# Two-layer convolution and retention block: paired projections computed by Strassen's seven products

## The chip, the cores and the metric

The kernel runs on one core of a Trainium2 chip. The metric is device time in microseconds from launch to end; a run's time is that of its slowest core, here the only one. TensorE (PE in the profile) multiplies, VectorE (DVE), ScalarE (ACT) and GpSimd (POOL) do elementwise work, and SyncE (SP) issues the transfers.

## The reference, cut to what matters

The program is two model blocks in one launch, all in float32, on 528 tokens (16 meta tokens and 512 of x) of 1024 features. The first block (attention and a gated recurrence, then a feed-forward part) is not touched. The second block runs two layers; in each, one wide projection of the normed input feeds a retention branch, a convolution branch and two gates:

```python
def _short_conv_branch(h, gb, gc, z, conv_w, conv_b, w_out):
    u = gc * h
    up = jnp.pad(u, ((0, 0), (CONV_WIDTH - 1, 0), (0, 0)))
    T = u.shape[1]
    y = conv_b + sum(conv_w[j] * up[:, j:j + T] for j in range(CONV_WIDTH))
    y = gb * y * jax.nn.silu(z)
    return y @ w_out
...
    for l in range(DEPTH_2):
        xn = _rmsnorm(h, pre_norm_g[l])
        proj = xn @ w_in[l] + b_in[l]
        c_h, c_b, c_c, c_z, r_q, r_k, r_v, r_z, g_a, g_b = jnp.split(proj, split_at, axis=-1)
        y_a = _short_conv_branch(c_h, c_b, c_c, c_z, conv_w[l], conv_b[l], w_conv_out[l])
        y_b = _retention_branch(r_q, r_k, r_v, r_z, ret_gn_g[l], w_ret_out[l])
        y = jax.nn.sigmoid(g_a) * y_a + jax.nn.sigmoid(g_b) * y_b
        y = y @ w_o[l]
        h = h + _rmsnorm(y, post_norm_g[l])
```

The convolution's four inputs (c_h, c_b, c_c, c_z) and the gates g_a and g_b are each 1024 features of `x_normed @ w_in + b_in`, so eight output tiles of 128 features apiece.

## The kernel before, in words

Activations lie transposed: features on the 128 partitions, tokens along the row, as eight "k tiles" of 128 features. A float32 product is made of three passes of TensorE's faster float32r form: every operand is split exactly in a high and a low part, and `mm3` adds high by high, high by low and low by high (L146 to L148). A **unit** is the weights of one output tile, 128 by 1024 numbers, 512 KB. `unit` (L123 to L125) loads it on SP's queue into one of three buffers `wraw`, ScalarE makes the high part `whi`, VectorE the low part `wlo` (three buffers each). These three instructions are given a priority 60 instructions ahead of where they stand. `proj` multiplies a unit by the tokens of a segment: 8 k tiles by 3 passes, 24 matmuls into one PSUM bank of the eight. `fproj` does so for each segment: in the first layer always two halves of 264 tokens; in the second, where the meta tokens' outputs don't count, one segment of 512, except for the two inputs of the convolution's product, which take segments of 258 and 256 tokens.

A planner (list scheduling at build time) sets the order on each engine: of the instructions whose inputs and buffers are ready it takes the one that stands first by priority, and it hands out whichever buffer of a kind is free. Semaphores then hold each engine to that order of its own.

Each layer has the retention branch first, then the stretch that the change touches, inside the pool `cv`: for each of eight convolution tiles four units (c_c, c_h, c_b, c_z) with their eviction (L1130 on ScalarE, L1136 on VectorE), the three-tap convolution on VectorE (L1138, L1140), the gates' products (L1145, L1149, L1150 on GpSimd) and the split of the result (L140, L141); then eight units g_b (sigmoid L1158 on ScalarE, product L1159 on GpSimd) and eight units g_a (L1163). After these the convolution's output projection (units `wc`, L1168 and L1169) is mixed with the retention output and split into the place of the layer's normed input `xs`, from which the last projection (`wo`) reads. In this stretch all is paced by the order of the projections on TensorE: 48 units per layer before `wc`. The first layer's stretch lies at 1223 to 1503 us of the profile, the second's at 2057 to 2325 us.

Of the kernel before, what the change touches and what calls it, by code (L numbers as in the profile page):

```python
# [7 lines left out]
F32 = mybir.dt.float32  # L8
# [29 lines left out]

# vector parameters: one column of 128 features each
# [18 lines left out]
class Builder:  # L58
# [5 lines left out]
    # ---------------------------------------------------------------- helpers  # L64
# [19 lines left out]
    # A chain is work whose steps wait for each other across the engines. It yields how many  # L84
    # projections to put on the tensor engine before its next step.
# [26 lines left out]
    def unit(self, src, pool=None):  # L112
        """One weight unit from DRAM, split exactly into two float32r parts; these stay in pool."""
        nc = self.nc
        cols = src.shape[-1]
        raw = self.wp.tile([P, 1040], F32, name="wraw", tag="wraw", bufs=3)[:, :cols]
        hi, lo = (
            (pool or self.wp).tile([P, 1024 if pool else 1040], F32R, name=f"w{n}", tag=f"w{n}", bufs=KEEP if pool else 3)[:, :cols]
            for n in ("hi", "lo")
        )  # L120
        # ahead of the work of the projections before it
        with self.tc.high_priority(offset=AHEAD):
            nc.sync.dma_start(raw, src)  # L123
# [13 lines left out]
    def split(self, hi, lo, src, eng=None):  # L137
        """src in two parts that float32r holds."""
# [4 lines left out]
    def mm3(self, out, w, x, start, stop):  # L143
        """out += w^T x from the exact two part splits of both."""
# [22 lines left out]
    def fproj(self, src, xs, segs, tick=True):  # L167
        """The same for a whole unit of 8 k tiles, for each segment of tokens."""
# [5 lines left out]

    def tokproj(self, xs, w0, us, n):
        """Rows of the token window at w0 times a chunk of n columns."""
# [26 lines left out]
    def metaproj(self, us, n):  # L203
        """The meta tokens' rows times a chunk."""
# [7 lines left out]
    def sqacc(self, acc, src, a, n, first, eng=None, last=False):  # L212
        """acc[:, a:a+n] (+)= src ** 2; the last square is returned instead of added."""
# [34 lines left out]
    def spread(self, r2, cols):  # L248
        """The same on all partitions, as a row, in PSUM."""
# [9 lines left out]
    def normed(self, src, g, dst, a, n, rb):  # L259
        """dst (hi, lo) = src times its norm factors rb times the weights g."""  # L260
# [13 lines left out]
    # ---------------------------------------------------------------- block 1  # L274
    def block1(self, stack):
# [4 lines left out]
        with tc.tile_pool(name="b1", bufs=1) as b1:  # L280
# [8 lines left out]
            # the attention's half of the output projection, by halves of the tokens: the first  # L289
            # half's norm runs under the second  # L290
# [16 lines left out]
    def out_proj(self, us, u, f, m, h, a, n):  # L307
        """h += an output tile of one branch's half of the output projection."""
# [4 lines left out]
    def mixer(self, b1, h, acc, mixh, fq, fk, lf8):  # L313
        """Both branches' outputs, before the output projection."""
# [7 lines left out]
        # h's place serves the recurrence's queries and gates until h is wanted  # L322
# [11 lines left out]
        rb = acc        # in its place, once the squares are summed  # L334
        W = [(w, P) for w in WIN1]
        with tc.tile_pool(name="lbp", bufs=1) as lp:
            # the input times the norm's weights; the norm's factors come with the projections' outputs
# [30 lines left out]
            # 1 - lower bound of the forget gate: cumsum(softmax over the one layer) - its first row  # L368
# [10 lines left out]
            for c in range(2):  # L379
# [3 lines left out]
                for t in (1, 2, 3, 4, 0):  # L383
# [13 lines left out]
                    for u, ps in todo:  # L397
# [4 lines left out]
                        # -f, away from 0  # L402
# [44 lines left out]
        # one step is a head's token tile; each runs in three stages, and projections between  # L447
        # them keep the tensor engine at work while the other engines are at a stage
# [74 lines left out]
    def hgrn_step(self, hc, hd, t, f, omf, V, qT, og, M, Mk, mask, mixh):  # L523
# [8 lines left out]
        if t < 4:  # L532
            # k of this tile, decayed to the tile's end
# [5 lines left out]
        if t > 0:  # L539
# [6 lines left out]
            for b in range(2):  # L546
# [6 lines left out]
                # level l's queries are the odd ones of the blocks of 64 >> l tokens, its keys the even ones  # L553
# [47 lines left out]
    def blocks(self, x, l, i):  # L601
        """The tile's blocks of 64 >> l tokens, every second from i."""
# [91 lines left out]
            # a step is a head's query tile: scores and softmax, later its transposes, then the head's output  # L694
# [51 lines left out]
    def fox_turn(self, t, hd, PT, PM, pt):  # L746
        """The tile's weights with the keys on the partitions."""
# [12 lines left out]
        if t == 3:  # L760
            # this tile meets only the last keys: their product goes whole
# [573 lines left out]
```

## Time and profile before

| | us |
|---|---|
| median of 3 runs (lowest, highest) | 2428.38 (2424.8, 2431.4) |
| span of the profiled execution | 2429.1 |
| TensorE busy in it | 2385.5 |
| VectorE busy | 1204.2 |
| ScalarE busy | 877.6 |
| GpSimd busy | 381.8 |

The span, from the first instruction to the last, is the profiled execution's own time; it lies 0.7 us above the median of the runs. Busy time counts the union of an engine's instructions. Matmuls are pipelined, so the durations of single matmuls overlap; what one costs is read from the distance between starts.

### The profile page before, as it was taken

The numbers are of one execution on the slowest core, as the hardware profiler recorded it, in microseconds if no ns is written. First come the engines' busy times: TensorE is split into PE (matmuls) and PEld (weight loads), VectorE is DVE, ScalarE is ACT, GpSimd is POOL, SyncE is SP. The second block draws the span as 40 slices with busy tenths as digits, with TensorE's granted clock in tenths as the row PEclk, the third lists the DMA queues.
The fourth block names the chain that finished last, engine by engine and source line by source line (L and its number), as shares of the span: only waits on it lengthen the run. The fifth ranks groups of instructions, "written<-read, shape, count | busy, mean of one in ns | idle before, by whom it ended". The sixth has DMA issues, their size and how long they took to land.

```text
span 2429.1 us, 38728 instructions
## 1 busy us (share of the span) xinstructions
PE 2385.5 (98%) x16130; PEld 2199.9 (91%) x16130; DVE 1204.2 (50%) x2131; ACT 877.6 (36%) x1522; POOL 381.8 (16%) x431
## 2 busy tenths in 40 slices
PE   8999989999999999999999999999999999999998
PEld 7888878888889999999999999999898888898888
DVE  5467776333337645455534323566455554443243
ACT  6333564222225434242422233454332323222223
POOL 3133442000004211110100020042110110001200
PEclk9999999999999999999999999999999999999999
DMA  4212103222334322222122222413222222222222
GB/s 159 90 33 67 62 20 120 95 93 93 94 120 165 109 88 74 82 79 87 62 96 87 93 91 87 131 66 116 82 81 86 87 83 73 93 96 96 96 87 70
DMA packets 67615, 217.87 MB, mean 90 GB/s; under 512 B 8816, under 2 KB 14576, under 8 KB 67440
## 3 DMA queue, kind: packets, MB, share of 16 engines
q1 hardware_dynamic: 67440, 215.40, 26.6%
q8 instruction: 126, 2.06, 0.3%
q14 instruction: 49, 0.40, 0.1%
HBM read 213.28 MB, written 2.10 MB: 89 GB/s over the span
## 4 chain that ended last, share of the span: by engine, by line
PE 92%; DVE 3%; POOL 2%; ACT 2%; issue 1%; DMA 0%; SPq 0%; DVEq 0%; ACTq 0%; POOLq 0%
PE ps L146 29%; PE ps L147 29%; PE ps L148 28%; PE ps L197 2%; POOL hacc L223 1%; PE ps L569 1%; PE ps L253 1%; PE ps L234 1%; PE ps L1018 0%; PE ps L550 0%; ACT whi L124 0%; DVE E L557 0%; PE ps L753 0%; DVE fst L734 0%; DVE wlo L125 0%
## 5 line engine op out<-in xcount | busy, mean ns | idle before, releaser
L124 ACT ACTIVATE whi<-wraw 128x1024 fp32r<-128x1024 f32 (+1 forms) x385 | 404.2, 1053 | 976.9 <-PE ps L147 733.5
L125 DVE TENSOR_TENSOR wlo<-wraw,whi 128x1024 fp32r<-128x1024 f32 (+1 forms) x385 | 474.8, 1236 | 507.1 <-ACT whi L124 491.7
L147 PE MATMUL ps<-xsl,whi 128*128 128x264 f32 (+2 forms) x1792 | 546.3, 305 | 2.0 <-POOL xsl L141 0.9
L146 PE MATMUL ps<-xsh,whi 128*128 128x264 f32 (+2 forms) x1792 | 546.8, 305 | 0.0
L148 PE MATMUL ps<-xsh,wlo 128*128 128x264 f32 (+2 forms) x1792 | 542.2, 303 | 0.0
L146 PE MATMUL ps<-xph,whi 128*128 128x512 f32 (+4 forms) x1208 | 393.5, 326 | 0.0
L148 PE MATMUL ps<-xph,wlo 128*128 128x512 f32 (+4 forms) x1208 | 392.2, 325 | 0.0
L147 PE MATMUL ps<-xpl,whi 128*128 128x512 f32 (+4 forms) x1208 | 391.6, 324 | 0.4
L147 PEld LDWEIGHTS ps<-xsl,whi 128*128 128x128 f32 x1792 | 337.0, 188 | 18.0 <-POOL xsl L141 2.9
L146 PEld LDWEIGHTS ps<-xsh,whi 128*128 128x128 f32 x1792 | 337.1, 188 | 14.9
L148 PEld LDWEIGHTS ps<-xsh,wlo 128*128 128x128 f32 x1792 | 337.6, 188 | 14.2
L147 PEld LDWEIGHTS ps<-xpl,whi 128*128 128x128 f32 x1208 | 227.1, 188 | 21.2 <-POOL xpl L141 1.0
L148 PEld LDWEIGHTS ps<-xph,wlo 128*128 128x128 f32 x1208 | 227.2, 188 | 20.0
L146 PEld LDWEIGHTS ps<-xph,whi 128*128 128x128 f32 x1208 | 227.3, 188 | 19.8
L241 POOL TENSOR_TENSOR rs<-rs,mhalf 88x3 f32<-88x3 f32 (+4 forms) x25 | 33.2, 1330 | 790.3 <-DVE rs L239 790.3
L147 PE MATMUL ps<-srl,whi 128*128 128x264 f32 (+1 forms) x384 | 123.2, 321 | 0.0
L146 PE MATMUL ps<-srh,whi 128*128 128x264 f32 (+1 forms) x384 | 123.2, 321 | 0.0
L148 PE MATMUL ps<-srh,wlo 128*128 128x264 f32 (+1 forms) x384 | 123.1, 321 | 0.0
L1150 POOL TENSOR_TENSOR y<-y,sz 128x528 f32<-128x528 f32 (+1 forms) x16 | 29.2, 1826 | 393.3 <-ACT sz L1149 393.3
L919 POOL TENSOR_TENSOR t<-t,t 128x264 f32<-128x264 f32 (+2 forms) x58 | 61.6, 1081 | 179.2 <-DVE t L918 179.1
L146 PE MATMUL ps<-acth,whi 128*128 128x512 f32 (+2 forms) x242 | 80.8, 334 | 0.0
L148 PE MATMUL ps<-acth,wlo 128*128 128x512 f32 (+2 forms) x242 | 80.5, 332 | 0.0
(345 smaller groups left out, 4375.7 us busy)
## 6 DMA issues: line engine op xcount, KB each, us to landing
wraw<-in_w SPq DMA_DIRECT2D x164, 512.0 KB, 3.3
wraw<-in_wv SPq DMA_DIRECT2D x40, 512.0 KB, 3.3
wraw<-in_wr SPq DMA_DIRECT2D x32, 512.0 KB, 3.2
wraw<-in_w_gate SPq DMA_DIRECT2D x24, 512.0 KB, 3.6
wraw<-in_w_up SPq DMA_DIRECT2D x24, 512.0 KB, 3.5
wraw<-in_w_down SPq DMA_DIRECT2D x22, 512.0 KB, 3.4
wraw<-in_wc SPq DMA_DIRECT2D x16, 512.0 KB, 3.2
wraw<-in_wo SPq DMA_DIRECT2D x16, 512.0 KB, 3.3
```

The source lines that it names most:

```text
L124: nc.scalar.activation(hi, raw, AF.Copy)
L125: nc.vector.tensor_tensor(lo, raw, hi.bitcast(F32), ALU.subtract)
L146: nc.tensor.matmul(out, w[0], x[0], start=start, stop=False)
L147: nc.tensor.matmul(out, w[0], x[1], start=False, stop=False)
L148: nc.tensor.matmul(out, w[1], x[0], start=False, stop=stop)
L197: self.nc.tensor.matmul(ps, x2[:, kt], us[kt // 4][w][:, c : c + n], start=kt == 0 and w == 0, stop=kt == KD - 1 and w == 1,)
L223: (eng or nc.vector).tensor_tensor(dst, dst, sq, ALU.add)
L234: nc.tensor.matmul(st[:n, j : j + 1], acc[:, a : a + n], self.ones, start=True, stop=sq is None)
L241: nc.gpsimd.tensor_tensor(r2[:m, :k], r[:m, :k], self.mhalf[:m, :k], ALU.pow)
L253: self.nc.tensor.matmul(rb[:, o : o + n], r2[:n, j : j + 1].to_broadcast([n, P]), self.ident[:n, :n], start=True, stop=True)
L919: nc.gpsimd.tensor_tensor(t1, t1, t2, op)
L1150: nc.gpsimd.tensor_tensor(y[:, q0:], y[:, q0:], sz[:, q0:], ALU.mult)
```

## The change

In each layer the convolution tiles from the third on (`PLAIN = 2` stay as they are) and both gates are no longer multiplied unit by unit, but in **pairs of units**: (c_c, c_h), (c_b, c_z) of a tile, and two neighbouring tiles of a gate. Two units and all tokens make a product of 2 by 2 blocks (two output tiles; the two halves of the features, 4 k tiles each; two halves of the tokens, 264 columns in the first layer and 258 in the second). A direct product takes eight block products, Strassen's scheme (in Winograd's form) seven. Twenty pairs per layer go this way.

For each pair `pair` loads two units, forms four sums of weight blocks on VectorE and splits seven blocks instead of four. The sums of the token blocks (`operands`) are made and split once per layer, beside the two plain tiles; one of the four (`x4`, for the product named m4) takes the place of a block of `xs`, and so is split after the last plain product. `seven` issues the products: 7 by 4 k tiles by 3 passes, 84 matmuls per pair, and postpones a pair's last two products into the next pair (`late`). `a` is a PSUM bank in which three sums build on each other; `keep` copies it to SBUF in between. `sink` combines PSUM and kept parts into the two output tiles `o0` and `o1`, and then adds bias and function, which before were part of the eviction. The g_a pairs alternate with the output projection, and the mixed result goes to `yb` first and is split to `xs` for six tiles together, then two.

```diff
+PLAIN = 2
+PAIRAHEAD = 130
...
+    def pair(self, sa, sb, pool):
...
+        def split(names, src, where):
+            n = src.shape[-1]
+            hi, lo = ((self.wp if where == "w" else pool).tile(
+                [P, 1040 if where == "w" else 1024], F32R, name=f"{where}{x}", tag=f"{where}{x}", bufs=3)[:, :n] for x in ("hi", "lo"))
+            nc.scalar.activation(hi, src, AF.Copy)
+            nc.vector.tensor_tensor(lo, src, hi.bitcast(F32), ALU.subtract)
...
+        with self.tc.high_priority(offset=PAIRAHEAD):
+            ra, rb = (self.wp.tile([P, 1040], F32, name="wraw", tag="wraw", bufs=3)[:, :1024] for _ in range(2))
+            nc.sync.dma_start(ra, sa)
+            nc.sync.dma_start(rb, sb)
+            split(("a11", "a12"), ra, "w")
+            s23, s14 = (pool.tile([P, 1056], F32, name="ws", tag="ws", bufs=2) for _ in range(2))
...
+            nc.vector.tensor_tensor(s1, a21, a22, ALU.add)
+            nc.vector.tensor_tensor(s2, s1, a11, ALU.add)
+            nc.vector.tensor_tensor(s3, a21, a11, ALU.add)
+            split(("s2", "s3"), s23[:, : 2 * H], "s")
+            nc.vector.tensor_tensor(s4, s2, a12, ALU.add)
+            split(("s1", "s4"), s14[:, : 2 * H], "s")
+            split(("a22",), a22, "w")
...
+    def seven(self, units, X, n, pool):
...
+        def keep(ps):
+            t = pool.tile([P, HB], F32, name="keep", tag="keep", bufs=4)[:, :n]
+            nc.scalar.activation(t, ps, AF.Copy)
+            return t
...
+        for sa, sb, sink in units:
+            w = self.pair(sa, sb, pool)
+            a = self.ps()[:, :n]
+            prod(a, w["a11"], X["m1"], True)
+            m1 = keep(a)
+            d = self.ps()[:, :n]
+            prod(d, w["a12"], X["m2"], True)
+            sink(0, 0, d, m1)
+            if late:
+                last(*late, 0)
+            prod(a, w["s2"], X["n6"], False)
+            u = keep(a)
+            c = self.ps()[:, :n]
+            prod(c, w["s3"], X["m7"], True)
+            if late:
+                last(*late, 1)
+            prod(a, w["s1"], X["n5"], False)
+            sink(1, 1, c, keep(a))
+            late = a, c, u, w, sink
...
+            x4 = cv.tile([P, 1056], F32, name="ws", tag="ws", bufs=2)[:, : 4 * hn].rearrange("p (k n) -> p k n", k=4)
...
+            prep = self.start(operands())
+            for i in range(PLAIN):
...
+            self.finish(prep)
+            for kt in range(4):
+                self.split(X["m4"][0][:, kt], X["m4"][1][:, kt], x4[:, kt])
...
+                    if (i, h) == (0, 0):
+                        nc.vector.tensor_tensor(dst, ps, other, ALU.add)
+                    elif (i, h) == (0, 1):
+                        nc.scalar.activation(dst, ps, *func)
+                    else:
+                        nc.vector.tensor_tensor(dst, ps, other, ALU.subtract)
...
+            self.seven(pairs(), X, hn, cv)
+            self.seven(pairs_a(0, 4), X, hn, cv)
+            mixed(0, 2)
+            self.seven(pairs_a(4, 6), X, hn, cv)
+            mixed(2, 4)
+            self.seven(pairs_a(6, 8), X, hn, cv)
+            mixed(4, 6)
+            split_mixed(0, 6)
+            mixed(6, 8)
+            split_mixed(6, 8)
...
+    nc = bacc.Bacc("TRN2", target_bir_lowering=False, num_devices=1, dynamic_dma_scratch_size=1024)
```

## Rows read from the trace of the kernel before

**Rows 1.** Page, head and part 1: busy us (share of the span) xinstructions.
```profile
span 2429.1 us, 38728 instructions
...
PE 2385.5 (98%) x16130; PEld 2199.9 (91%) x16130; DVE 1204.2 (50%) x2131; ACT 877.6 (36%) x1522; POOL 381.8 (16%) x431
```
**Rows 2.** Stretches: us; PE, PEld, DVE, ACT, POOL busy (instructions); clock; DMA.
```profile
1223.00:1409.00 186.00, 186.00 (x1531) 186.00 (x1530) 75.75 (x104) 50.89 (x70) 13.62 (x7) 1.00 0.27 91
...
1409.00:1456.00 47.00, 47.00 (x388) 47.00 (x387) 10.52 (x9) 17.14 (x26) 15.89 (x8) 1.00 0.27 91
...
2057.00:2237.00 180.00, 180.00 (x1143) 162.79 (x1142) 72.22 (x88) 48.91 (x63) 11.94 (x7) 1.00 0.27 94
```
**Rows 3.** Waits, 1223 to 1549: waiter, releaser; total us, times, longest.
```profile
ACT whi L124 <- PE ps L147: 141.3, 47, 4.8
```
**Rows 4.** Timeline, PE, first layer's convolution: start us, us, instruction; 36 starts apart.
```profile
1299.79 0.28 PE L148 MATMUL ps<-xsh,wlo 128*128 128x264 f32 x1
...
1304.16 0.28 PE L148 MATMUL ps<-xsh,wlo 128*128 128x264 f32 x1
```
**Rows 5.** Timeline of PE, second layer's gates; 36 starts apart.
```profile
2290.00 0.40 PE L148 MATMUL ps<-xph,wlo 128*128 128x512 f32 x1
...
2298.34 0.40 PE L148 MATMUL ps<-xph,wlo 128*128 128x512 f32 x1
```
**Rows 6.** Timeline of PE, second layer's convolution; 8 and 18 starts apart.
```profile
2149.81 0.28 PE L147 MATMUL ps<-xpl,whi 128*128 128x256 f32 x1
...
2150.75 0.29 PE L146 MATMUL ps<-xph,whi 128*128 128x258 f32 x1
...
2152.93 0.29 PE L146 MATMUL ps<-xph,whi 128*128 128x258 f32 x1
```
**Rows 7.** DVE groups, 1223 to 1503: count, busy us, mean ns, idle before.
```profile
L125 DVE TENSOR_TENSOR wlo<-wraw,whi 128x1024 fp32r<-128x1024 f32 x48 | 58.8, 1224 | 126.9 <-ACT whi L124 126.9
...
L1140 DVE SCALAR_TENSOR_TENSOR y<-u,vec,y 128x528 f32<-128x528 f32 x16 | 12.2, 766 | 0.3
...
L141 DVE TENSOR_TENSOR xpl<-y,xph 128x528 fp32r<-128x528 f32 x8 | 5.7, 708 | 15.1 <-ACT xph L140 15.1
...
L1138 DVE TENSOR_SCALAR y<-u,vec 128x528 f32<-128x528 f32 x8 | 4.4, 555 | 0.3
...
L1086 DVE TENSOR_TENSOR yb<-ps,yb 128x264 f32<-128x264 f32 x1 | 0.4, 433 | 1.0 <-PE ps L148 1.0
```
**Rows 8.** Groups by form, DVE, 2057 to 2325.
```profile
L141 DVE TENSOR_TENSOR xpl<-y,xph 128x512 fp32r<-128x512 f32 x8 | 5.5, 692 | 14.8 <-ACT xph L140 14.8
```
**Rows 9.** Groups by form, ACT, 1223 to 1503.
```profile
L124 ACT ACTIVATE whi<-wraw 128x1024 fp32r<-128x1024 f32 x48 | 50.9, 1061 | 139.8 <-PE ps L147 130.4 <-issue 9.4
...
L140 ACT ACTIVATE xph<-y 128x528 fp32r<-128x528 f32 x8 | 5.2, 646 | 16.8 <-POOL y L1150 16.8
```
**Rows 10.** Timeline of DVE with a full queue, first layer's convolution.
```profile
1305.44 0.56 DVE L1138 TENSOR_SCALAR y<-u,vec 128x528 f32<-128x528 f32 x1
1305.91 1.22 DVE L125 TENSOR_TENSOR wlo<-wraw,whi 128x1024 fp32r<-128x1024 f32 x1
1307.05 1.57 DVE L1140 SCALAR_TENSOR_TENSOR y<-u,vec,y 128x528 f32<-128x528 f32 x2
1308.72 0.49 DVE L1145 SCALAR_TENSOR_TENSOR y<-ps,vec,y 128x264 f32<-128x264 f32 x1
```
**Rows 11.** Timelines of DVE and POOL where both read two SBUF operands.
```profile
1270.77 1.23 DVE L125 TENSOR_TENSOR wlo<-wraw,whi 128x1024 fp32r<-128x1024 f32 x1 [4.59 <-ACT whi L124]
...
1271.18 2.00 POOL L1150 TENSOR_TENSOR y<-y,sz 128x528 f32<-128x528 f32 x1 [21.35 <-ACT sz L1149]
...
1945.21 3.52 POOL L919 TENSOR_TENSOR t<-t,t 128x512 f32<-128x512 f32 x2 [12.66 <-DVE t L918]
...
1945.71 1.88 DVE L125 TENSOR_TENSOR wlo<-wraw,whi 128x1024 fp32r<-128x1024 f32 x1
```
**Rows 12.** Page, part 6: DMA issues xcount, KB each, median us to landing.
```profile
wraw<-in_w SPq DMA_DIRECT2D x164, 512.0 KB, 3.3
```

More of the change, by code (lines that the diff above doesn't have):

```diff
@@ L173, in fproj @@
                 self.tick()
+    def pair(self, sa, sb, pool):
+        nc = self.nc
+        H = 512
+        parts = {}
+        def split(names, src, where):
[4 more added lines that the diff above has]
+            nc.vector.tensor_tensor(lo, src, hi.bitcast(F32), ALU.subtract)
+            for j, name in enumerate(names):
+                parts[name] = (hi[:, j * H : j * H + H], lo[:, j * H : j * H + H])
+        with self.tc.high_priority(offset=PAIRAHEAD):
[4 more added lines that the diff above has]
+            s23, s14 = (pool.tile([P, 1056], F32, name="ws", tag="ws", bufs=2) for _ in range(2))
+            s1, s2, s3, s4 = s14[:, :H], s23[:, :H], s23[:, H : 2 * H], s14[:, H : 2 * H]
+            a11, a12, a21, a22 = ra[:, :H], ra[:, H:], rb[:, :H], rb[:, H:]
+            nc.vector.tensor_tensor(s1, a21, a22, ALU.add)
[5 more added lines that the diff above has]
+            split(("a22",), a22, "w")
+        return parts
@@ new lines, in seven, with prod, last @@
+    def seven(self, units, X, n, pool):
+        nc = self.nc
+        late = None
+        def prod(ps, w, x, first):
+            for kt in range(4):
+                wk = tuple(y[:, kt * P : kt * P + P] for y in w)
+                xk = tuple(y[:, kt] for y in x)
+                for i, (p, q) in enumerate(((0, 0), (0, 1), (1, 0))):
+                    nc.tensor.matmul(
+                        ps, wk[p], xk[q], start=first and kt == 0 and i == 0, stop=kt == 3 and i == 2, skip_group_check=True
+                    )
+        def keep(ps):
+            t = pool.tile([P, HB], F32, name="keep", tag="keep", bufs=4)[:, :n]
+            nc.scalar.activation(t, ps, AF.Copy)
+            return t
+        def last(a, c, u, w, sink, part):
+            if part == 0:
+                prod(a, w["s4"], X["m3"], False)
+                sink(0, 1, a, None)
+            else:
+                prod(c, w["a22"], X["m4"], False)
+                sink(1, 0, c, u)
+        for sa, sb, sink in units:
[17 more added lines that the diff above has]
+            late = a, c, u, w, sink
+        last(*late, 0)
+        last(*late, 1)
@@ L1142, in layer2, with conv_out @@
                     )
+                return y
+            def conv_out(i, y, sz):
+                nc.gpsimd.tensor_tensor(y[:, q0:], y[:, q0:], sz[:, q0:], ALU.mult)
+                self.split(ych[:, i, q0:], ycl[:, i, q0:], y[:, q0:])
+            prep = self.start(operands())
+            for i in range(PLAIN):
+                g, b = fp("c_c", i, OUTC)
+                cc = tile_("o0")
+                for ps, a, n in g:
+                    nc.scalar.activation(cc[:, a : a + n], ps, AF.Identity, bias=b)
+                g, b = fp("c_h", i, OUTC)
+                u = tile_("u", 1, 2)
+                if not last:
+                    nc.vector.memset(u[:, 0:2], 0.0)
+                for ps, a, n in g:
+                    nc.vector.scalar_tensor_tensor(u[:, 2 + a : 2 + a + n], ps, b, cc[:, a : a + n], ALU.add, ALU.mult)
+                y = conv(i, u)
                 g, b = fp("c_b", i, OUT)
@@ L1160, in layer2 @@
-            for i in range(KD):
-                gen, b = fp("g_a", i, OUT)
-                for ps, a, n in gen:
-                    nc.scalar.activation(ga[:, i, a : a + n], ps, AF.Sigmoid, bias=b)
-            for i in range(KD):
-                for ps, a, n in self.fproj(d[f"wc{l}"][i], (ych, ycl), OUTH if i == KD - 1 else OUT):
-                    t = cv.tile([P, NT], F32, name="mt", tag="y", bufs=2)[:, :n]
-                    nc.vector.tensor_tensor(t, ps, ga[:, i, a : a + n], ALU.mult)
-                    nc.vector.tensor_tensor(t, t, yb[:, i, a : a + n], ALU.add)
-                    self.split(xh[:, i, a : a + n], xl[:, i, a : a + n], t)
+                conv_out(i, y, sz)
@@ new lines, in layer2, with sink, f @@
+            self.finish(prep)
+            for kt in range(4):
+                self.split(X["m4"][0][:, kt], X["m4"][1][:, kt], x4[:, kt])
+            def sink(bias, func, done):
+                o = [tile_("o0"), tile_("o1")]
+                def f(i, h, ps, other):
+                    dst = o[i][:, HALF[h]]
+                    if (i, h) == (0, 0):
+                        nc.vector.tensor_tensor(dst, ps, other, ALU.add)
+                    elif (i, h) == (0, 1):
+                        nc.scalar.activation(dst, ps, *func)
+                    else:
+                        nc.vector.tensor_tensor(dst, ps, other, ALU.subtract)
+                    if (i, h) == (1, 0):
+                        done(*o)
+                return f
@@ new lines, in layer2, with conv_in, done @@
+            ys = {}
+            all_ = slice(t1, t2 + hn)
+            def conv_in(i):
+                def done(cc, ch):
+                    u = tile_("u", 1, 2)
+                    if not last:
+                        nc.vector.memset(u[:, 0:2], 0.0)
+                    nc.scalar.activation(cc[:, all_], cc[:, all_], AF.Identity, bias=B(col["c_c"] + i))
+                    nc.vector.scalar_tensor_tensor(
+                        u[:, 2 + t1 : 2 + t2 + hn], ch[:, all_], B(col["c_h"] + i), cc[:, all_], ALU.add, ALU.mult
+                    )
+                    ys[i] = conv(i, u)
+                return sink(None, (AF.Copy,), done)
@@ new lines, in conv_gate, with done, gates @@
+            def conv_gate(i):
+                def done(cb, cz):
+                    y = ys[i]
+                    nc.vector.scalar_tensor_tensor(y[:, q0:], cb[:, q0:], B(col["c_b"] + i), y[:, q0:], ALU.add, ALU.mult)
+                    nc.scalar.activation(cz[:, q0:], cz[:, q0:], AF.Silu, bias=B(col["c_z"] + i))
+                    conv_out(i, y, cz)
+                return sink(None, (AF.Copy,), done)
+            def gates(name, i, use):
+                def done(*o):
+                    for j in range(2):
+                        nc.scalar.activation(o[j][:, q0:], o[j][:, q0:], AF.Sigmoid, bias=B(col[name] + i + j))
+                    use(i, o)
+                return sink(None, (AF.Copy,), done)
@@ new lines, in gated_b, with pairs @@
+            def gated_b(i, o):
+                for j in range(2):
+                    nc.gpsimd.tensor_tensor(yb[:, i + j, q0:], yb[:, i + j, q0:], o[j][:, q0:], ALU.mult)
+            ga = {}
+            def pairs():
+                for i in range(PLAIN, KD):
+                    yield w[wu["c_c"] + i], w[wu["c_h"] + i], conv_in(i)
+                    yield w[wu["c_b"] + i], w[wu["c_z"] + i], conv_gate(i)
+                for i in range(0, KD, 2):
+                    yield w[wu["g_b"] + i], w[wu["g_b"] + i + 1], gates("g_b", i, gated_b)
@@ new lines, in pairs_a, with mixed @@
+            def pairs_a(i0, i1):
+                for i in range(i0, i1, 2):
+                    yield w[wu["g_a"] + i], w[wu["g_a"] + i + 1], gates("g_a", i, ga.__setitem__)
+            def mixed(i0, i1):
+                for i in range(i0, i1):
+                    for ps, a, n in self.fproj(d[f"wc{l}"][i], (ych, ycl), OUTH if i == KD - 1 else OUT):
+                        t = cv.tile([P, NT], F32, name="mt", tag="y", bufs=1)[:, :n]
+                        nc.vector.tensor_tensor(t, ps, ga[i // 2 * 2][i % 2][:, a : a + n], ALU.mult)
+                        nc.vector.tensor_tensor(yb[:, i, a : a + n], t, yb[:, i, a : a + n], ALU.add)
@@ new lines, in split_mixed @@
+            def split_mixed(i0, i1):
+                for i in range(i0, i1):
+                    self.split(xh[:, i, q0:], xl[:, i, q0:], yb[:, i, q0:])
+            self.seven(pairs(), X, hn, cv)
[8 more added lines that the diff above has]
+            split_mixed(6, 8)
```

59 lines of the change are left out of this document (36 added, 23 removed).

## Prediction

> **What bounds the kernel now.** I read the page's head first: TensorE is busy 98% of the span, VectorE half, ScalarE a third [rows 1]. A share of busy time says little about one stage, so the stretches come next: in the convolution and gate stretches of both layers TensorE is busy in every microsecond at a granted clock of 1.00, the 2.4 GHz level, while VectorE works about 40% (75.75 of 186 us) in the convolution and 22% (10.52 of 47) under the gates [rows 2]. The waits of the first layer's stretch confirm it: the longest on the weight path is ScalarE's, for buffers that TensorE gives back, 141 us in 47 times; none of the 17 lines of that view has TensorE as the waiter [rows 3]. So TensorE's instruction stream sets the time there, and a matmul removed is time saved, as long as nothing else becomes later than TensorE.
>
> **What a matmul costs** is the distance of starts, not its recorded length. With 264 columns: 4.37 us over 36 starts, 121.4 ns [rows 4]. With 512: 8.34 over 36, 231.7 ns [rows 5]. With 256: 0.94 over 8, 117.5 ns; with 258: 2.18 over 18, 121.1 ns [rows 6].
>
> **Removed.** First layer: a pair took 2 units x 24 matmuls x 2 halves = 96 and takes 84 now, both with 264 columns: 12 x 0.1214 = 1.46 us less, over 20 pairs 29.1 us. A pair now takes 10.20 us. Second layer: the pair (c_c, c_h) took 48 of 258 and 48 of 256, 11.45 us; 84 of 258 take 10.17, so 1.28 less, six times: 7.7 us. The other 14 pairs took 48 of 512, 11.12 us, so 0.95 less each: 13.3 us. There the gain is smaller because short matmuls cost more per column. Together **50.1 us**, all on the path that sets the end.
>
> **Added on VectorE.** A pair prepares three splits of 1024 columns (1.224 each), one of 512 (0.692) and four sums of 512 (taken as 0.692, the same operation and width): 7.13 us [rows 7, 8]. Its three combinations from PSUM cost 0.433 each, 1.30 [rows 7]. The convolution's own work stays: three at 0.766 and one at 0.555 in the first pair of a tile (2.85; the memset of two columns is left aside), 0.766 + 0.708 in the second (1.47) [rows 7]. A tile (two pairs, 28 instructions) is 14.26 + 2.60 + 2.85 + 1.47 = 21.2 us by recorded durations, against 20.4 us of TensorE. That is the crux: **VectorE goes from 40% to about TensorE's own time.**
>
> What it really needs is bounded from both sides. With a full queue the next instruction starts before the recorded end of the one in front: 1.14 us after the start of a 1.22 us split, 0.47 after that of a 0.56 us one [rows 10]. At 0.09 less each, 28 instructions take 18.7 us. Where one needs the other's result, two of 0.766 take 1.67 [rows 10], 0.07 more each; if all 28 paid that, 23.2 us. GpSimd adds to both: its product of 1271.18 takes 2.00 us of which the first 0.82 passes until VectorE's split ends, so 1.18 us is its own; and a split that starts while GpSimd works is stretched, 1.88 us against 1.22 [rows 11]. One such product per tile makes 19.9 to 24.4 us. I take 10 of the 28 as dependent (the second weight sum and the convolution's three steps are; the others hang on ScalarE's copies, mostly done by then): 18.7 + 10 x 0.16 = 20.3, and the whole 1.2 for GpSimd: 21.5 us, nearer to the packed end, as a saturated queue is packed. That is 1.1 us over TensorE, on 12 tiles **13 us** (bounds 0 and 48).
>
> The Trainium skill's page "SBUF — State Buffer", section "Who interferes with whom", says that a VectorE instruction with two SBUF inputs and a GpSimd instruction that reads SBUF exclude each other for a whole instruction. The stretched rows agree. Without that exclusion the tile would be 20.3 us, below TensorE's 20.4, and the 13 us would be nothing.
>
> In the g_b pairs GpSimd has two products: 8.43 by durations, about 7.75 packed with two dependents, plus 2.36, is 10.1 us against 10.2 of TensorE (bounds 9.8 and 11.6); I take 0.2 us for each of the 8, **2 us** (0 to 11). The g_a pairs have 8.43 at most and cost nothing.
>
> **Added on ScalarE and the queues.** Per pair 3 x 1.061 + about 0.63 for the high parts, four copies out of PSUM and one or two whole tiles at no more than 0.65 each [rows 9]: 7.7 us at most, under 10.2; nothing. SP issues the same transfers, 1 MB per 10.2 us instead of per 11.6; one lands in 3.3 us [rows 12], and the three raw buffers turn over once the sums and the first split are done, some 5 us into a pair. Nothing, unless VectorE's backlog passes that.
>
> **Waits at the seams.** At the start of the paired stage `x4` holds one of the two `ws` buffers, so the first pair's weight sums wait until the last plain product is done and its four splits follow: about 0.4 + 4 x 0.43 = 2.1, three sums 2.1, the high copy 1.06 [rows 7 to 9]: 5.3 us, 6.5 with the low part. The first two products cover 2.9 us, the next pair's first two, if the planner pulls them forward, 2.9 more. So 0 to 3.6 per layer, I take 2: **4 us**. Queued behind this on VectorE are the combinations of the same pair, which nobody needs earlier. Each of the four calls of `seven` per layer ends without a following pair; its last two products wait for a copy (ScalarE, under 0.65) with no cover but the next projections. The last split of the mixed tile now spans 528 columns, and the final projection's first 21 matmuls (2.5 us) cover its chain of some 2.4. 0 to 1.2 for each of eight ends, I take 0.5: **4 us** (0 to 10). The sums of the token blocks (44 VectorE instructions of about 0.43, 19 us) lie beside the two plain tiles, where VectorE has 60% free in 46 us: nothing.
>
> **Sum.** Added 13 + 2 + 4 + 4 = 23 us, removed 50.1. The profiled execution takes 2429.1 us [rows 1], 0.7 above the median of 2428.4; 2429.1 - 27.1 = 2402.0, less 0.7 gives **2401 us**.
>
> **Rivals.** (1) VectorE becomes the plain bound: every instruction pays its full recorded duration, 21.2 + 1.2 = 22.4 us per tile. For it: such an engine stands in order, and any late hand-off blocks the combinations behind it. Against: the starts ahead of the recorded end in [rows 10]. Price: 2.0 x 12 = 24, the g_b pairs 0.6 x 8 = 5, seams 8: 37 us back, 2415 (2410 to 2428). The Trainium skill's page "VectorE: DVE Perf Modes", section "The DRAIN you can't avoid", speaks for it: the next instruction does not start until the pipe has emptied. The rows here show a start 0.09 us before the recorded end.
>
> (2) Slower: split weights come too late in every pair. A pair holds one of three `whi`/`wlo` buffers for its a22 block until late in the next pair, so the next a11/a12 must take the buffer given back after the second product, 2.9 us into a pair of 10.2. If it gets only the one that is given back after the sixth, one product (1.46 us) covers 1.06 + 1.22 and half an instruction of queue on both engines, 3.4 us: TensorE waits 1.9 us in each of 40 pairs, 78 us, and VectorE then has time: 2428.4 - 50.1 + 78 = 2456. It decides from 1.25 us per pair on (50.1 / 40). Against it: the planner gives out whichever buffer is free. For it: three raw buffers for two units per pair, and a VectorE that is nearly full.
>
> (3) VectorE keeps up (19.9 us): only seams cost, 2382 to 2386.
>
> That 84 matmuls replace 96 can be counted in the code; I keep no chance for less.
>
> **How the numbers follow.** Chances: 0.55 for the forecast (2390 to 2410), 0.22 for (1), 0.12 for (3), 0.11 for (2). A measurement of this kernel tells about 0.3%, 7 us, from no change: faster means under 2421. The forecast, (3) and three quarters of (1) lie there: 0.83; the rest of (1) and a little of (2) within 0.3%: 0.07; slower 0.10. The range 2382 to 2424 holds the forecast, nearly all of (1) and half of (3).
>
> **What would show it.** In the changed profile: distances of starts of 121 ns with 258 and 264 columns; 192 matmuls more in all (240 and 72 fewer where segments were halves, 504 more where they were 512 wide), on the 16130 recorded before [rows 1]; VectorE busy over 90% in the convolution's stretch and about 80% under the gates; a paired convolution tile near 21.5 us, a pair of a gate near 10.2. TensorE's waits should name VectorE (combinations and low parts) in the convolution and hardly anything under g_a. Waits on `whi` or on transfers at the head of every pair would mean rival (2); PE without gaps in the convolution, rival (3). The prediction is wrong if the short matmuls cost another distance in the new order, or if VectorE needs over 23 us per tile.

## The result, and the profile after

The changed kernel takes **2389.4 us** (median of 4 runs, 2386.2 to 2395.1) against 2429.6 for the kernel before (4 runs, one more than above). The ratio is 0.9842 [0.9825, 0.9859], 1.6% faster. The profiled span fell by 40.7 us. Of the 50.1 us that the prediction removed, 9.4 came back, not the 23 that it added up. One run of one experiment below (e2_gates_only, 8154.69 us) is left out as slow.

The page's head and first part of the changed kernel, which answer to [rows 1]:

```profile
span 2388.4 us, 40000 instructions
...
PE 2338.1 (98%) x16322; PEld 2177.8 (91%) x16322; DVE 1453.8 (61%) x2560; ACT 999.6 (42%) x1751; POOL 374.8 (16%) x431
```

TensorE has 192 matmuls more and 47.4 us less busy time; VectorE has 249.6 us more. The stretches, as in [rows 2] (length; busy us and instructions of PE, PEld, DVE, ACT, POOL; granted clock; DMA): tokens and plain tiles, paired convolution, g_b, then g_a and the mixed tile of the first layer; then the paired convolution of the second.

```profile
1223.00:1270.00 47.00, 47.00 (x388) 47.00 (x387) 35.24 (x76) 17.77 (x32) 1.94 (x1) 1.00 0.21 72
1270.00:1392.00 122.00, 121.26 (x990) 120.70 (x989) 116.17 (x171) 73.50 (x115) 8.14 (x6) 1.00 0.32 109
1392.00:1433.00 41.00, 41.00 (x338) 41.00 (x337) 38.81 (x51) 25.80 (x40) 11.04 (x6) 1.00 0.30 102
1433.00:1523.00 90.00, 88.27 (x716) 87.24 (x715) 55.27 (x84) 38.46 (x57) 5.33 (x4) 1.00 0.28 95
...
2079.00:2203.00 124.00, 123.76 (x1027) 123.02 (x1026) 117.56 (x171) 73.42 (x118) 8.54 (x6) 1.00 0.31 105
```

VectorE is at 95% in the convolution (116.17 of 122), where it was at 41% before, and TensorE still loses only 0.74 us there. TensorE's timeline confirms it at full length: the same matmul of two pairs (start, length), ten pairs and 840 starts apart.

```profile
1303.03 0.28 PE L223 MATMUL ps<-xsh,shi 128*128 128x264 f32 x1
...
1405.56 0.28 PE L223 MATMUL ps<-xsh,shi 128*128 128x264 f32 x1
```

102.53 / 840 = 122.1 ns a matmul, 10.25 us a pair, against 121.4 in [rows 4]: no gap opens between matmuls here. Six pairs of the second layer, 504 starts apart:

```profile
2097.00 0.28 PE L223 MATMUL ps<-xph,shi 128*128 128x258 f32 x1
...
2157.38 0.28 PE L223 MATMUL ps<-xph,shi 128*128 128x258 f32 x1
```

That is 119.8 ns a matmul and 10.06 us a pair. All waits of TensorE that name a paired line, and those of the mixed tile, from the view of the whole run (waiter, releaser; total us, times, longest):

```profile
PE ps L223 <- DVE o L1302: 3.0, 3, 1.3
...
PE ps L149 <- DVE xpl L143: 1.0, 1, 1.0
...
PE ps L223 <- ACT keep L229: 0.9, 1, 0.9
...
PE ps L148 <- ACT xph L142: 0.2, 1, 0.2
```

They stand at five places (us): 1286 (second pair of the stage), 1436.7 and 1455.7 (ends of two calls of `seven` in the first layer), 2239.6 (the same in the second), and 2329 (last split of the mixed tile). No line names `whi` or a transfer.

Counted from the first eviction of the convolution to the first square behind the block, the first layer took 328.0 us and takes 304.6, a gain of 23.4 of the 29.1 removed. The second took 322.4 and takes 304.2: 18.1 of 21.0. The tail behind it is 1.2 us longer, and what lies before and between gives 0.3.

### The profile page after: what moved, and what is told of

The parts are those of the page before. It is cut to its first block, busy times and chain, and to the rows that moved or that the text cites. A ratio compares the mean times of both kernels' runs of the same rounds, so it can differ in the third digit from the quotient of the medians.

```text
span 2388.4 us, 40000 instructions
## 1 busy us (share of the span) xinstructions
PE 2338.1 (98%) x16322; PEld 2177.8 (91%) x16322; DVE 1453.8 (61%) x2560; ACT 999.6 (42%) x1751; POOL 374.8 (16%) x431
## 4 chain that ended last, share of the span: by engine, by line
PE 87%; DVE 6%; ACT 2%; POOL 2%; issue 2%; DMA 1%; SPq 0%; DVEq 0%; ACTq 0%; POOLq 0%
PE ps L148 23%; PE ps L149 23%; PE ps L150 22%; PE ps L223 13%; PE ps L284 2%; POOL hacc L310 1%; PE ps L656 1%; PE ps L340 1%; PE ps L321 1%; DMA wraw<-in_w 1%; PE ps L1105 0%; DVE wlo L189 0%; PE ps L637 0%; ACT whi L126 0%; DVE slo L189 0%
## 5 line engine op out<-in xcount | busy, mean ns | idle before, releaser
L149 PE MATMUL ps<-xsl,whi 128*128 128x264 f32 (+2 forms) x1152 | 364.5, 317 | 1.8 <-POOL xsl L143 0.9
L148 PE MATMUL ps<-xsh,whi 128*128 128x264 f32 (+2 forms) x1152 | 365.6, 317 | 0.0
L150 PE MATMUL ps<-xsh,wlo 128*128 128x264 f32 (+2 forms) x1152 | 361.5, 314 | 0.0
L148 PE MATMUL ps<-xph,whi 128*128 128x264 f32 (+4 forms) x792 | 251.4, 317 | 0.2 <-ACT xph L142 0.2
L149 PE MATMUL ps<-xpl,whi 128*128 128x264 f32 (+4 forms) x792 | 249.9, 316 | 1.4 <-DVE xpl L143 1.0
L150 PE MATMUL ps<-xph,wlo 128*128 128x264 f32 (+4 forms) x792 | 249.5, 315 | 0.0
L149 PEld LDWEIGHTS ps<-xsl,whi 128*128 128x128 f32 x1152 | 217.2, 189 | 17.7 <-POOL xsl L143 2.7
L148 PEld LDWEIGHTS ps<-xsh,whi 128*128 128x128 f32 x1152 | 217.4, 189 | 15.1 <-ACT xsh L142 0.2
L150 PEld LDWEIGHTS ps<-xsh,wlo 128*128 128x128 f32 x1152 | 217.5, 189 | 14.2
L189 DVE TENSOR_TENSOR slo<-ws,shi 128x1024 fp32r<-128x1024 f32 x80 | 102.9, 1296 | 10.7 <-ACT shi L188 10.3
```

Of the source, the lines that this page charges most:

```text
L148: nc.tensor.matmul(out, w[0], x[0], start=start, stop=False)
L149: nc.tensor.matmul(out, w[0], x[1], start=False, stop=False)
L150: nc.tensor.matmul(out, w[1], x[0], start=False, stop=stop)
L189: nc.vector.tensor_tensor(lo, src, hi.bitcast(F32), ALU.subtract)
```

## The experiments

Each was timed beside the kernel before on the same chip (2428.7 to 2428.9 us). "On the changed kernel" is against its own time, 2389.4, or 2388.4 where it was run once more (e9).

### The size of a product, and of the two parts

**e1_eight**: the a12 product is issued twice, so a pair has 96 matmuls again.

```diff
             prod(d, w["a12"], X["m2"], True)
+            prod(d, w["a12"], X["m2"], True)
```

> The scheme as in the changed kernel, but with the product of a12 made twice in every pair, so eight block products instead of seven; the outputs do not change. If TensorE's stream still sets the time in the paired stretches, each of 20 pairs per layer grows by 12 matmuls: 12 x 0.122 x 20 = 29 us in the first layer, 12 x 0.120 x 20 = 29 us in the second, together +58 us on the changed kernel (about 2447, slower than before by 18). If VectorE sets it in the convolution (24 of 40 pairs) with some room behind it, those pairs hide part of the added products: +25 to +45 us.

2441.66 us (2440.84 to 2447.52), ratio 1.0054 [1.0035, 1.0073]: 52 us on the changed kernel, between the two cases expected. Of the 58 us that 480 matmuls take, 52 appear. The other 6 are in part shorter waits (1.0 us in the first layer, 2.5 in the changed kernel). So time in these stretches goes with TensorE's instructions nearly in full, which speaks against VectorE's 95% as the bound.

**e2_gates_only**: all convolution tiles plain.

```diff
-PLAIN = 2
+PLAIN = 8
```

> All eight convolution tiles as before; only the gates go by seven products. Theory (TensorE's stream sets the time): the gates alone are worth 8 x 1.46 + 8 x 0.95 = 19.3 us against the kernel before, less 4 to 7 us at seams: 2414 to 2418. If instead VectorE limits the paired convolution tiles, the convolution had brought little, and the gates alone come near the changed kernel: 2393 to 2405.

2415.01 us (median of three, 2413.77 to 2417.76), 0.9948 [0.9927, 0.9968]: 13.9 us gained by the medians, 12.6 by the ratio.

**e3_conv_only**: both gates by plain products. The gates read a block of `xs` that an operand of the convolution has replaced, so their values differ; their work is the same.

```diff
...
-            self.seven(pairs_a(0, 4), X, hn, cv)
+            plain_gates("g_b", 0, 8, gated_b)
+            plain_gates("g_a", 0, 4, ga.__setitem__)
...
-            self.seven(pairs_a(4, 6), X, hn, cv)
+            plain_gates("g_a", 4, 6, ga.__setitem__)
...
-            self.seven(pairs_a(6, 8), X, hn, cv)
+            plain_gates("g_a", 6, 8, ga.__setitem__)
```

> Convolution tiles from the third on in pairs, both gates as before. Theory: the convolution's pairs are worth 12 x 1.46 + 6 x (1.28 + 0.95) = 30.8 us against the kernel before, less 3 to 6 us at seams: 2403 to 2407. VectorE as the limit at 21.5 us per tile, as predicted: 13 us less of that, 2413 to 2420.

2402.11 us (2399.67 to 2405.61), 0.9893 [0.9875, 0.9912]: 26.8 us gained. The two parts give 39 to 41 us, the whole 40: they add up, and the convolution, where the prediction put most of the loss, carries two thirds of the gain.

### How near VectorE is to its limit

**e4_more_vector**: in the 24 pairs of the convolution one low part of 1024 columns is computed twice.

```diff
...
-            split(("s1", "s4"), s14[:, : 2 * H], "s")
+            hi, lo = split(("s1", "s4"), s14[:, : 2 * H], "s")
+            if more:
+                nc.vector.tensor_tensor(lo, s14[:, : 2 * H], hi.bitcast(F32), ALU.subtract)
...
```

> In the convolution's 24 pairs one low part of 1024 columns is computed twice on VectorE, 1.14 us more per pair, nothing else changes. Theory (VectorE stands just under TensorE, idle 5.8 us in the 12 pairs of the first layer's 122 us, 0.5 us per pair): 0.6 to 0.7 us of it shows, +16 us on the changed kernel (about 2405). If VectorE sets the time there already: all of it, +27 us (2417). If VectorE has real room: under +5 us.

2420.17 us (2414.39 to 2427.03, 10 runs), 0.9964 [0.995, 0.9977]: 31 us (25 to 38 by single runs), all of the 27 us of VectorE's work that was added, and by the median more. The execution in the trace is the fastest of the ten.

**e11_more_vector_half**: the same with 512 columns, 0.6 us a pair.

```diff
...
+                nc.vector.tensor_tensor(lo[:, :H], s1, hi[:, :H].bitcast(F32), ALU.subtract)
...
```

> As e4, but the repeated low part has 512 columns, 0.6 us more of VectorE per pair in the convolution's 24 pairs. Theory of a threshold (VectorE has about 0.5 us per pair free, doubling GpSimd's product took it to 98% busy at no cost in time): 0 to +5 us on the changed kernel. If e4's cost goes in proportion to the work added (24 to 31 us for 1.14 us): +13 to +16 us.

2404.1 us (2401.06 to 2406.61), 0.9897 [0.9883, 0.9911]: 15.7 us, about all of the added work (24 x 0.6 = 14.4). That looks as if VectorE had no room at all.

**e5_less_vector**: the low part of a22 isn't computed (that of s4 stands in for it), 0.6 us less in all 40 pairs.

```diff
+            if names == ("a22",):
+                hi = self.wp.tile([P, 1040], F32R, name="whi", tag="whi", bufs=3)[:, :n]
+                nc.scalar.activation(hi, src, AF.Copy)
+                parts["a22"] = (hi, parts["s4"][1])
+                return
```

> The low part of the a22 block is not computed (its place in the products is taken by the low part of s4, so the results are not the reference's; all transfers, products and copies stay): 0.6 us less of VectorE in each of 40 pairs. If VectorE is what costs the changed kernel its last microseconds (doubling a low part in 24 pairs cost 24 to 31 us, and eight products instead of seven cost 52 where the count alone says 58), the waits of TensorE for the combinations go: -4 to -7 us on the changed kernel, 2382 to 2386. If TensorE's stream alone sets the time and the loss lies in the seams: within 2 us of the changed kernel.

2391.67 us (2390.01 to 2393.17), 0.9851 [0.9834, 0.9867]: nothing gained for 24 us less work. The edit also moved hand-offs: TensorE waits 4.8 us in the first layer, for 2.5 in the changed kernel, 2.6 of them at once for a `keep` copy (1411).

**e6_pool_twice**: a second, unused product on GpSimd behind the first, to hold VectorE up longer.

```diff
                 nc.gpsimd.tensor_tensor(y[:, q0:], y[:, q0:], sz[:, q0:], ALU.mult)
+                nc.gpsimd.tensor_tensor(sz[:, q0:], y[:, q0:], sz[:, q0:], ALU.mult)
```

> GpSimd makes a second product of the same size behind that of the convolution's result in every convolution tile (32 SBUF-to-SBUF products of 528 or 512 columns instead of 16; nothing uses the second). If GpSimd and VectorE exclude each other for the whole of such a product (the 1.2 us of the prediction) and VectorE has no time left, +1.2 us per paired tile, 14 us (2403). At the stretch seen in the changed profile, 0.5 us per product, +6 us (2395). If GpSimd costs VectorE nothing, no change. The split behind the product may also start later; nothing waits for it in this stretch.

2390.07 us (2385.74 to 2392.49), 0.984 [0.9825, 0.9855]: no change beyond the spread. VectorE's instructions are stretched by 9.7 us in the first layer's convolution (durations above the changed kernel's median of the same shape; 3.3 us there), it is busy 98% (119.68 of 122), and ten steady pairs still take 102.53 us. TensorE is busy 120.30 us of the 122, for 121.26.

**Read together**, these four speak against a bound by VectorE's total time: 98% costs about nothing (e6: 6.4 us more of stretch in 12 pairs), less than 95% gives nothing (e5), and yet 0.6 us more in a pair, 7.2 in 12, costs its full price (e11), though VectorE then idles 6 of the 122 us (115.91 busy). What differs is in the traces of GpSimd's product, which multiplies the convolution's result `y` by its gate; `xph` and `xpl` are the high and low part made of it (start, us, instruction [idle before <- releaser]). First the changed kernel, GpSimd and then VectorE:

```profile
1344.75 1.33 POOL L1262 TENSOR_TENSOR y<-y,o 128x528 f32<-128x528 f32 x1 [19.30 <-ACT o L1328]
...
1344.35 0.43 DVE L1302 TENSOR_TENSOR o<-ps,keep 128x264 f32<-128x264 f32 x1
1344.69 0.43 DVE L1298 TENSOR_TENSOR o<-ps,keep 128x264 f32<-128x264 f32 x1
1345.07 0.06 DVE L1315 MEMSET u<- 128x2 f32 x1
1345.60 1.57 DVE L189 TENSOR_TENSOR wlo<-wraw,whi 128x1024 fp32r<-128x1024 f32 x1 [0.47 <-ACT whi L188]
```

The product begins under the combinations, which read one operand from PSUM and keep their 0.43 us; only the split behind them is stretched, by 0.35. In e4:

```profile
1306.63 3.99 POOL L1265 TENSOR_TENSOR y<-y,o 128x528 f32<-128x528 f32 x1 [34.96 <-DVE slo L189]
...
1305.37 2.35 DVE L189 TENSOR_TENSOR slo<-ws,shi 128x1024 fp32r<-128x1024 f32 x2
1307.64 0.68 DVE L189 TENSOR_TENSOR wlo<-wraw,whi 128x512 fp32r<-128x512 f32 x1
1308.24 1.21 DVE L209 TENSOR_TENSOR slo<-ws,shi 128x1024 fp32r<-128x1024 f32 x1
1311.33 0.71 DVE L143 TENSOR_TENSOR xpl<-y,xph 128x528 fp32r<-128x528 f32 x1 [1.87 <-ACT xph L142]
1311.95 0.43 DVE L1305 TENSOR_TENSOR o<-ps,keep 128x264 f32<-128x264 f32 x1
...
1310.65 0.64 ACT L142 ACTIVATE xph<-y 128x528 fp32r<-128x528 f32 x1 [3.23 <-POOL y L1265]
```

VectorE has moved by the added work, and the product falls on a row of instructions with both inputs in SBUF. It lasts until 1310.62, 1.2 us behind the last of them (L209, the added one). ScalarE's copy `xph` waits 3.23 us for it, VectorE's low part waits 1.87 us for that copy with the combination L1305 behind it, and TensorE waits 2.8 us for the combination, the longest of the waits in this line of e4 (1266 to 1433):

```profile
PE ps L226 <- DVE o L1305: 11.0, 7, 2.8
```

Each engine takes its instructions in the planned order, so one late product stops three engines. In e11 it is the same with another end: a product of 3.25 us at 1390.85, `xph` 3.0 us late, and behind it on ScalarE the `keep` copy for which TensorE waits (1220 to 1560):

```profile
PE ps L226 <- ACT keep L232: 5.4, 5, 3.2
PE ps L226 <- DVE o L1305: 2.6, 4, 1.4
```

The waits of ScalarE for the product, 1266 to 1433, in the changed kernel, e6, e11 and e4:

```profile
ACT xph L142 <- POOL y L1262: 4.1, 6, 1.4
```
```profile
ACT xph L142 <- POOL y L1262: 3.8, 6, 1.4
```
```profile
ACT xph L142 <- POOL y L1265: 13.4, 7, 3.0
```
```profile
ACT xph L142 <- POOL y L1265: 14.9, 7, 3.2
```

e6 leaves the first product at 1.33 us (median of 7); the second, 2.19 us, has nobody waiting for it. e11 has a median of 2.14, e4 of 2.28. So, by these rows, the price is that of a hand-off moved onto other work, not of VectorE's load. The Trainium skill's page "SBUF — State Buffer", section "Who interferes with whom", has a rule for it: a VectorE instruction with at most one SBUF input, outside its two-port modes, does not contend with GpSimd; one with two contends with a GpSimd instruction that reads SBUF; and the shared port pair is an exclusive lock. The rows agree: 0.43 beside the product is 0.43 without, and 1.33 us become 3.99 behind two-input instructions.

This reading rests on the traces. A kernel that takes `y`'s product off GpSimd in e11's place would have shown it by itself; it was not run. Nor does the wait for the product give the whole size: e8 (below) has 12.9 us of it in the same stretch and costs only 10. The size is in TensorE's starts. What they lie further apart than usual (122 ns with 264 columns, 120 with 258) adds up, over both layers' stretches (1223 to 1560 and 2030 to 2400), to 10.9 us in the changed kernel, 14.3 in e6, 14.8 in e5, 20.3 in e8, 26.8 in e11 and 39.1 in e4. e11's 15.9 more is its 15.7 us; e6 and e5 lose some 3 to 4 us more there than the changed kernel, which the medians hardly show.

### The seams, and the planner's reach

**e7_carry**: the last two products of a call of `seven` are carried into the next call.

```diff
...
-            self.seven(pairs(), X, hn, cv)
-            self.seven(pairs_a(0, 4), X, hn, cv)
+            late = self.seven(pairs(), X, hn, cv, None, False)
+            late = self.seven(pairs_a(0, 4), X, hn, cv, late, False)
...
-            self.seven(pairs_a(4, 6), X, hn, cv)
+            late = self.seven(pairs_a(4, 6), X, hn, cv, late, False)
...
-            self.seven(pairs_a(6, 8), X, hn, cv)
+            self.seven(pairs_a(6, 8), X, hn, cv, late, True)
```

> The last two products of a pair are carried over from one call of the pairs' loop into the next, so that only the last pair of a layer ends without a follower: three of four seams per layer go. TensorE waits 1.0 + 1.0 us at them in the first layer and 1.5 + about 0.5 us in the second, so -2 to -5 us on the changed kernel (2384 to 2387) if seams cost what the waits say; no change if the waits only move to the next hand-off of a full VectorE.

2384.52 us (2382.42 to 2389.18), 0.9822 [0.9807, 0.9837]: 4.9 us better than the changed kernel (3.9 against e9), by the medians; the intervals of the ratios overlap.

**e9_changed_again** is the changed kernel once more, beside the next three.

> The changed kernel unaltered, as the partner on the same chip for the other three runs: 2389 us, 0.984 of the kernel before.

2388.4 us (2385.94 to 2389.81), 0.9832 [0.9818, 0.9845].

**e10_carry_split**: e7, and the last two tiles of the mixed stage are split segment by segment.

```diff
...
+                        if split:
+                            self.split(xh[:, i, a : a + n], xl[:, i, a : a + n], yb[:, i, a : a + n])
...
-            mixed(6, 8)
-            split_mixed(6, 8)
+            mixed(6, 8, True)
```

> The carried products of e7, and the last two tiles of the mixed result are split segment by segment as in the kernel before, so the final projection's first products need not wait for a split of a whole tile (1.2 us of TensorE's wait in the second layer). If waits are worth what they show: 4 to 6 us under the changed kernel on the same chip (2383 to 2385). If e7's difference was the spread of runs: within 2 us.

2382.92 us (2381.59 to 2388.11), 0.981 [0.9797, 0.9824]: 5.5 us better than e9 by the medians, the fastest version here; the intervals overlap a little. Of TensorE's waits for the paired block this is left, in the whole run:

```profile
PE ps L222 <- DVE o L1303: 0.9, 1, 0.9
...
PE ps L222 <- ACT keep L228: 0.3, 1, 0.3
```

TensorE's starts too far apart come to 3.8 us in both layers, for 10.0 in e9. So some 5 to 6 of the 9.4 us lost were the ends of the calls and the last split.

**e12_plain_1**: e10 with one plain tile in place of two.

```diff
-PLAIN = 2
+PLAIN = 1
```

> As e10, with one plain convolution tile instead of two. Two more pairs per layer are worth 2 x 1.46 + 1.28 + 0.95 = 5.1 us; but the sums of the token blocks (19 us of VectorE) then have 23 us of TensorE instead of 46 beside them, with 9 us of VectorE's own work and the first pair's sums. If VectorE finishes them in time: 5 us under e10. If TensorE waits for them at the first pair's third product: 4 to 10 us per layer come back, 3 to 15 us over e10.

2390.32 us (2389.15 to 2392.37), 0.9842 [0.9828, 0.9855]: 7.4 us worse than e10, although two more pairs per layer save some 5 us of TensorE's work by the prediction's prices (as many matmuls in all, 16322: 24 fewer in the first layer, and 24 more but shorter ones in the second). Its waits of TensorE, whole run, and its stretches around 1248:

```profile
PE ps L222 <- issue: 12.6, 2, 6.4
```
```profile
1240.00:1248.00 8.00, 8.00 (x66) 7.81 (x65) 7.93 (x21) 5.08 (x12) 1.37 (x1) 1.00 0.01 2
1248.00:1254.00 6.00, 0.03 (x1) 0.00 (x0) 3.75 (x7) 1.59 (x2) 1.71 (x1) 0.75 0.00 0
1254.00:1258.00 4.00, 3.79 (x17) 3.74 (x18) 3.86 (x5) 1.68 (x3) 0.00 (x0) 0.52 0.70 266
```

VectorE is full with the token blocks' sums until 1248 (7.93 of 8 us); the first weight sums come behind them, behind a wait for `xph`, and TensorE stands for 6 us in each layer. In e10 the second plain tile covers those 19 us.

**e8_ahead_60**: the planner may pull a pair's preparation forward by less.

```diff
-PAIRAHEAD = 130
+PAIRAHEAD = 60
```

> A pair's loads, sums and splits get a priority 60 instructions ahead instead of 130, so under one pair (84 matmuls). If the lead carries the scheme (rival 2's mechanism: split weights too late), TensorE waits at the head of pairs: 0.5 to 2 us in each of 40 pairs, +20 to +80 us (2410 to 2470). If the planner fills a nearly full VectorE in much the same order, or orders by readiness anyway: within 5 us of the changed kernel.

2399.2 us (2396.11 to 2404.48), 0.9882 [0.9866, 0.9897]: 10 us worse. TensorE's waits, 1266 to 1433, do not name the weights:

```profile
PE ps L223 <- ACT keep L229: 4.4, 5, 1.5
```

It is the same hand-off again: GpSimd's product lasts 2.41 us (median of 7), and ScalarE's `keep` copies stand behind `xph`.

## Why the prediction was right, point by point

The sign, the bound and the range held: 2389.4 lies in 2382 to 2424. The forecast, 2401, was 12 us too high. The time lies just below its own 2390 to 2410 and between it and rival (3), and the trace is that of (3): VectorE keeps up. So the range was right and the forecast's own reason, a VectorE that sets the convolution's time, was not; the range held because it reached down to (3). (It holds all of (3)'s 2382 to 2386, not half, as the prediction says.)

- **Removed, 50.1 us: right.** 192 matmuls more in all, as counted. A pair took 10.25 us where 10.20 was said (122.1 ns a start for 121.4), and 10.06 in the second layer for 10.17 (119.8 for 121.1). The 121.1 came from 18 starts; over the whole stretch of the kernel before it is 120.3 with 258 columns, 118.0 with 256 and 121.7 with 264. With these the work removed is 28.7 us in the first layer and 23.1 in the second, for 29.1 and 21.0: 51.8 in all. e1 puts a product back and pays 52 of 58; e2 and e3 give 12.6 to 13.9 and 26.8.
- **VectorE in the convolution, 13 us: mis-sized, it cost about nothing.** This is the step that failed. VectorE's busy time per tile is 116.17 / 122 x 20.5 = 19.5 us, not 21.5. The packed sum of 18.7 held, but two additions did not. Ten dependents at 0.16 were charged; the rows show none of it, since the planner's order puts an independent sum between s2 and s4, each 0.60 after the last, as packed as the others:

```profile
1284.94 0.69 DVE L202 TENSOR_TENSOR ws<-ws,wraw 128x512 f32<-128x512 f32 x1
1285.54 0.69 DVE L203 TENSOR_TENSOR ws<-wraw 128x512 f32<-128x512 f32 x1
1286.14 0.69 DVE L205 TENSOR_TENSOR ws<-ws,wraw 128x512 f32<-128x512 f32 x1
```

  And GpSimd's product was charged with 1.2 us; it stretched VectorE by 3.27 us for six in that stretch, 0.54 each, because much of it runs beside combinations out of PSUM or while VectorE idles. 18.7 + 0.5 makes 19.2 us a tile, against 20.5 of TensorE.
- **g_b pairs, 2 us: in effect nothing.** VectorE was stretched more there (5.6 us by six products), and TensorE was busy in all of the first layer's 41 us.
- **Seams, 4 + 4 us: near in sum (some 6.5), wrong in place.** The first pair's 2 us per layer was 0.9 in the first and some 0.5 in the second. The ends cost 1.0 + 1.0 in the first layer, 1.5 + 1.6 in the second; e7 and e10 took some 5.5 us of all this back.
- **The rest**: TensorE's starts that lie too far apart add up to 4.9 us in the first layer's stretch and 6.0 in the second's (0 and 0.3 in the kernel before). Half of the first is the three waits named (2.5 us), the rest are holes of 0.1 to 0.4 us. 51.8 less 10.6 is 41.2, against 40.7 measured. What the last line of the change, `dynamic_dma_scratch_size`, is worth by itself was not tested.
- **Rival (1)**, plain bound at 22.4 a tile, is out: a start 0.60 after a 0.69 us sum is ahead of the recorded end. The Trainium skill's page "VectorE: DVE Perf Modes", section "The DRAIN you can't avoid", has the next instruction wait until the pipe is empty, but adds that one which isn't held starts earlier; the rows show the second, and the prediction gave only the first. **Rival (2)**, late weights, is out: no wait for them in any pair, and with the planner's reach halved (e8) still none. A late hand-off was near all the same, but elsewhere: 0.6 us more of VectorE's work in a pair costs 15.7 us (e11), through the order of VectorE, GpSimd and ScalarE and not through the weights' buffers. The prediction did not see that.
- **What would show it**: VectorE is over 90% in the convolution, as said (95%); under the gates, where about 80% was said, it is at 95% with g_b (38.81 of 41) and at 61% over g_a and the mixed tile. Waits of TensorE that name VectorE in the steady convolution did not come.

## What to carry to other kernels

Here trading TensorE's time for VectorE's paid with VectorE at 95% of the stretch, fed in an order in which independent work stands between dependents: price such work by the distance of starts, not by recorded lengths. What then broke first was, by the traces, not the total but a hand-off: look in the trace for the one instruction on a third engine on which ScalarE, VectorE and TensorE stand in turn, and for what it runs beside. Charge each end of a pipelined group for its last product, and carry it into the next group.

## What the hardware showed that was not expected

- GpSimd's product of 528 columns takes 1.33 us beside combinations out of PSUM and up to 3.99 behind two-input splits. In both rows the later of the two was the one stretched: VectorE's split at 1345.60 (1.57 for 1.22) and GpSimd's product at 1306.63.
- One long wait costs more than itself. In e11 TensorE stood 3.18 us at 1391.9; the next 24 matmuls started 220 ns apart, not 121, 2.4 us more. The granted clock of those stretches:

```profile
1380.00:1392.00 12.00, 12.00 (x101) 12.00 (x99) 12.00 (x18) 5.90 (x9) 1.15 (x1) 1.00 0.26 89
1392.00:1395.00 3.00, 0.21 (x2) 0.00 (x1) 1.14 (x2) 0.86 (x3) 2.10 (x1) 0.87 0.54 175
1395.00:1399.00 4.00, 3.61 (x16) 3.61 (x17) 3.04 (x6) 1.90 (x4) 0.00 (x0) 0.50 0.00 0
```

  0.50 is the 1.2 GHz level. The same kernel's waits of 2.2 us and less were followed by 1.00, and so were all of the changed kernel's in this block. The length of the wait doesn't settle it: a longer wait in e4 was followed by starts 122 ns apart, a shorter one in e5 by eleven of 220 ns. The first matmul behind each, e4 and then e5:

```profile
1312.43 0.39 PE L226 MATMUL ps<-xsh,whi 128*128 128x264 f32 x1 [2.76 <-DVE o L1305]
```
```profile
1411.38 0.59 PE L228 MATMUL ps<-n5h,shi 128*128 128x264 f32 x1 [2.57 <-ACT keep L234]
```
